# The bank that carries four of the seven products, and one pair more done by seven products

## The chip, the cores and the metric

The kernel runs on one core of one Trainium2 chip. The metric is the device time of one execution in microseconds; before the change three runs gave 1723.54, 1724.14 and 1728.85 us, median 1724.14.

## What is computed

Two layers of an encoder trunk over 512 positions of width 1024. Each layer is a block of four token mixers with a gated sum and an output projection, and then a SwiGLU feed-forward of inner width 2816. Only the feed-forward changes:

```
h2 = rmsnorm(x, ln_ffn[l])
g_part, u_part = jnp.split(h2 @ w_gate_up[l], 2, axis=-1)
x = x + (jax.nn.silu(g_part) * u_part) @ w_down[l]
```

All is float32 in and out. TensorE's operands are float32r, so each matrix is split into a high and a low part (the high part by ScalarE's copy, L121, the low part by VectorE's subtraction, L122), and each product is the sum of three matmuls: high·high, high·low, low·high.

## The kernel before

The activations lie transposed, features on partitions and the 512 positions in the free dimension. The inner width 2816 is 22 tiles of 128. For each tile j the kernel makes a **pair**: the gate tile and the up tile, each 128 x 512, and from them silu(gate)·up, split into ah and al. After pairs 0 to 7, 8 to 15 and 16 to 21 (three groups) the 8 output tiles of the down projection each take their sum over the group's pairs into bank d, and VectorE adds d to x.

The string SEVEN says how pair j is made. An **ordinary** pair (`eight`) is two products of a 128 x 1024 weight tile with all of h: 48 matmuls of 512 columns. A pair **by seven** (`seven`) takes gate and up as two block rows, the contraction's two halves as block columns, and h as 2 x 2 blocks (halves of the contraction by halves of the positions), and forms the result of the eight block products from seven, with sums of weight blocks (s1 to s4) and of blocks of h (T1 to T4): 7 products of 4 x 3 matmuls of 256 columns, 84 in all. In both versions a11·B11 is part of three of the four results. The products go to three PSUM banks, which the traces call fa (r1), fb (r2) and fc (r3).

`sums(j)` loads and prepares the weights of a pair by seven: raw holds a11 and a12 (L1076), s31 is loaded plainly (L1078) and then added to in place by a second DMA, issued by POOL (L1081), and a22 is loaded (L1080). VectorE adds s24 from s31 and raw in two instructions. The splits are called `one` (from raw), v24 (from s24), v1 and v3 (the two halves of s31) and v22 (from a22). s31 and raw have two buffers each, so the load of pair n+2 waits until the last reader of pair n's tile is done; for s31 that is the split v3. In the trace s31, s24 and their splits appear as s_f, the splits of halves as vh_f and vl_f, of whole tiles as wh_f and wl_f.

`seven(j)` doesn't end its own pair: its last two products, a22·T4 and s4·B22, and what follows them are kept as `finish` and run by `rest()` in the middle of the next pair, or at the end of a group. Engines are in order. A scheduler orders the instructions of each engine when the kernel is built, by its own estimates and with `sums` raised in priority by AHEAD instructions, so where an instruction ends up isn't where the code has it.

Of the kernel before, what the change touches and what calls it, by code (L numbers as in the profile page):

```python
# [11 lines left out]
F32 = mybir.dt.float32  # L12
# [3 lines left out]
AF = mybir.ActivationFunctionType  # L16
# [3 lines left out]
P = 128  # L20
S = 512
# [7 lines left out]
LOG_EXP = "natural_log_exp_and_others"  # L29
WL, WR = 3, 2  # L30
LAYERS = range(L)
SEVEN = "8888887777777777777777"
AHEAD = 156
ORDER = "ccbccchhhchhcbchcghcchcchzccczccbccccccchgcgccchbbbcbhcgbzcbbcbccbgghcbgcgcbcccghchghchzhbccccbccccgcccccczhgcgbgchcgcccccccggggggbgcggggbcbbggcbbcbhcccbccbccccccccccccccccccbchccgbgggbchcbbbbbbhbbb"
PE = 8
# [27 lines left out]
def body(tc, io):  # L63
    nc = tc.nc
    V, A, T = nc.vector, nc.scalar, nc.tensor
# [5 lines left out]
    with pool("const") as cl, pool("hp") as hp, pool("wp", WL) as wp, pool("vals", side="right") as cp, \  # L71
# [30 lines left out]
        def tmp(shape, tag="t", dt=F32, bufs=None, name="t"):  # L102
            return tp.tile(shape, dt, tag=tag, name=name, bufs=bufs)

        def acc_psum(name="g"):
            return pm.tile([P, S], F32, tag="mm", name=name)
# [7 lines left out]
        def mul(out, a, b):  # L114
            V.tensor_tensor(out, a, b, op=ALU.mult)

        def add(out, a, b):
            V.tensor_tensor(out, a, b, op=ALU.add)  # L118

        def split(hi, lo, src):  # L120
            A.activation(hi, src, AF.Copy)  # L121
            V.tensor_tensor(lo, src, hi.bitcast(F32), op=ALU.subtract)  # L122
# [78 lines left out]
        def gemm(w, hh, hl, name, ready=None):  # L201
            hi, lo = ready or weight(w, 1024, name)
            ps = acc_psum(name)
            for k in range(KD):
                c = slice(k * P, (k + 1) * P)
                mm3(ps, hi[:, c], lo[:, c], hh[k], hl[k], k == 0, k == KD - 1)
            return ps
# [19 lines left out]
        for l in LAYERS:  # L227
# [14 lines left out]
            with pool(f"mo{l}") as mo, pool(f"mx{l}") as mp:  # L242
# [52 lines left out]
                for nm, c0 in (("m", PK_MR), ("d", PK_DR)):  # L295
                    t = cp.tile([P, 2, NT, 2, 32], F32, tag="rot" + nm, name=f"rot{nm}{l}")
# [715 lines left out]
                for nt in range(KD):  # L1012
                    ps = gemm(io["w_o"][l, nt], mh, ml, f"o{nt}", wo.get(nt))
# [6 lines left out]
            with pool(f"fa{l}") as fa, pool(f"ff{l}") as fp, ps_pool(f"fr{l}", 2) as fr:  # L1020
                tc.keep_in_program_order(nc.scalar.preload_act_table_set(LOG_EXP))
                hh, hl, scale, _ = prenorm(pk[:, PK_FFN:PK_FFN + 8], f"f{l}")
                H, Q = S // 2, KD // 2
# [29 lines left out]
                def moving(b, k):  # L1053
                    if b < 4:
                        return th[k][:, b], tl[k][:, b]
                    k, c = ((k, slice(0, H)), (k + Q, slice(0, H)), (k + Q, slice(H, S)))[b - 4]
                    return hh[k][:, c], hl[k][:, c]

                T1, T2, T3, T4, B11, B21, B22 = range(7)

                def product(ps, w, b, first):
                    for k in range(Q):
                        c = slice(k * P, (k + 1) * P)
                        bh, bl = moving(b, k)
                        for n, (lh, rh) in enumerate(((w[0], bh), (w[0], bl), (w[1], bh))):
                            T.matmul(ps[:, :H], lh[:, c], rh, start=first and k == 0 and n == 0,  # L1066
                                     stop=k == Q - 1 and n == 2, skip_group_check=True)
# [39 lines left out]
                def rest():  # L1107
                    for f in left:
                        f()
                    left.clear()  # L1110

                def hidden(j, g, u, sign=1.0):

                    V.scalar_tensor_tensor(u, u, sign, g, op0=ALU.mult, op1=ALU.mult)
                    ah[j] = fa.tile([P, S], F32R, tag=f"ah{j % 8}", name=f"ah{j}")
                    al[j] = fp.tile([P, S], F32R, tag=f"al{j % 8}", name=f"al{j}")
                    split(ah[j], al[j], u)

                def seven(j):
                    a11, a12, a22, s1, s2, s3, s4 = sums(j)  # L1120
                    gs = fp.tile([P, S], F32, tag="gs", name="gs")
                    us = fp.tile([P, S], F32, tag="us", name="us", bufs=2)
                    r1 = acc_psum(f"fa{j}")
                    product(r1, a11, B11, True)
                    c1 = tmp([P, H], "ps", name="c1")
                    A.activation(c1, r1[:, :H], AF.Copy)
                    rest()
                    r2 = fr.tile([P, S], F32, tag="r2", name=f"fb{j}")
                    r3 = acc_psum(f"fc{j}")
                    uu = tmp([P, 2, H], "n0", name="uu", bufs=1)  # L1130
                    product(r2, s2, T2, True)
                    add(uu[:, 0], c1, r2[:, :H])
                    product(r3, s1, T1, True)
                    product(r1, a12, B21, False)
                    A.activation(gs[:, :H], r1[:, :H], AF.Silu)
                    product(r2, s3, T3, False)
                    add(uu[:, 1], c1, r2[:, :H])
                    add(us[:, H:], uu[:, 1], r3[:, :H])

                    def finish():  # L1140
                        product(r2, a22, T4, False)
                        add(us[:, :H], c1, r2[:, :H])
                        product(r3, s4, B22, False)
                        add(gs[:, H:], uu[:, 0], r3[:, :H])
                        A.activation(gs[:, H:], gs[:, H:], AF.Silu)
                        hidden(j, gs, us, -1.0)

                    left.append(finish)

                def eight(j):  # L1150

                    t = [fp.tile([P, S], F32, tag=n, name=n, bufs=b) for n, b in (("gs", 1), ("us", 2))]
                    pr = []
                    for i in range(2):
                        if 2 * j + i < len(raw):
                            mul(t[i], raw[2 * j + i], r)
                            pr.append(t[i])
                        else:
                            pr.append(gemm(half_gu(2 * j + i), hh, hl, f"f{2 * j + i}"))
                        rest()  # L1160
                    A.activation(t[0], pr[0], AF.Silu)
                    if pr[1] is not t[1]:
                        mul(t[1], pr[1], t[0])
                        ah[j] = fa.tile([P, S], F32R, tag=f"ah{j % 8}", name=f"ah{j}")
                        al[j] = fp.tile([P, S], F32R, tag=f"al{j % 8}", name=f"al{j}")
                        split(ah[j], al[j], t[1])
                    else:
                        hidden(j, t[0], t[1])

                def half_gu(i):  # L1170
                    return io["w_gu"][l, i // 2, :, i % 2 * D:(i % 2 + 1) * D]
# [7 lines left out]
                for k0 in range(0, KF, 8):  # L1179
                    m = min(8, KF - k0)  # L1180
                    for j in range(k0, k0 + m):
                        (seven if SEVEN[j] == "7" else eight)(j)
                        if j < Q:
                            right_sums(j, r)
                    rest()
                    for nt in range(KD):
                        ps = acc_psum(f"d{nt}")
                        hi, lo = weight(io["w_d"][l, nt, :, k0 * P:(k0 + m) * P], m * P, f"d{nt}")
                        for j in range(m):
                            c = slice(j * P, (j + 1) * P)  # L1190
                            mm3(ps, hi[:, c], lo[:, c], ah[k0 + j], al[k0 + j], j == 0, j == m - 1)
                        add(x[nt], x[nt], ps)
                        if k0 + m == KF:
                            nc.sync.dma_start((io["out"] if l == L - 1 else xs)[nt], x[nt])
# [45 lines left out]
def layout(inp):  # L1240
# [9 lines left out]
    def tiles(a, n):  # L1250
# [18 lines left out]
    gu = gu.transpose(0, 2, 3, 1, 4).reshape(L, KF, P, 4, D // 2)  # L1269
    o["w_gu"] = np.stack([gu[:, j][:, :, [1, 0, 2, 3] if SEVEN[j] == "7" else [0, 1, 2, 3]]  # L1270
                          for j in range(KF)], 1).reshape(L, KF, P, 2 * D)
# [41 lines left out]
```

## Time and profile before

| what | value |
|---|---|
| median of three runs | 1724.14 us |
| the profiled execution | 1724.95 us |
| its span, first to last instruction | 1723.2 us |
| instructions | 25722 |
| TensorE's granted clock in the feed-forward stage, 655 to 730 us | 1.00 |
| first matmul of the feed-forward in layer 0 | at 511.87 us |
| pairs by seven | 16 a layer, 32 in all |

The page gives busy time by engine; "idle before" is time in which an engine waited, with what ended most of the wait. A matmul's duration overlaps the next one's, since they are pipelined: how fast TensorE works is read from the distance between starts. In a timeline row the first number is the start in us, the second the duration, and a bracket holds the idle time before it and what released it. SPq and POOLq are the queues that issue DMAs.

### The profile page before, as it was taken

What the parts mean: (1) busy time and instruction counts of PE and PEld (TensorE: products, weight loads), DVE (VectorE), ACT (ScalarE), POOL (GpSimd) and SP (SyncE); (2) the same over time, 40 slices, a digit from 0 to 9 for tenths busy, and PEclk for the clock granted to TensorE, in tenths of its full rate; (3) what the DMA queues carried; (4) which work ended last, traced back from release to release, by engine and by line L of the source; (5) the groups of instructions that cost most, each with busy time, mean ns of one, the idle gap of its engine ahead of it and who ended that gap; (6) DMA issues with size and microseconds to landing.
All of it is one profiled execution on the core that took longest, in us unless ns stands there. A gap on an engine that the chain in (4) does not pass through costs nothing.

```text
span 1723.2 us, 25722 instructions
## 1 busy us (share of the span) xinstructions
PE 1697.8 (99%) x10220; PEld 1422.5 (83%) x10220; DVE 1179.0 (68%) x1979; ACT 808.8 (47%) x1352; POOL 43.0 (2%) x68
## 2 busy tenths in 40 slices
PE   8999999999999999999999999999999999999999
PEld 6787778877787989989887777788777788899897
DVE  8858775457769647748677687754667695487473
ACT  7374353456555424525453743534564453254251
POOL 1000000000000000000000000000000000000000
PEclk9999999999999999999999999999999999999999
DMA  5222203332262435644442221142323624365443
GB/s 193 64 80 86 74 26 115 105 99 86 87 201 100 138 110 161 170 122 126 133 136 58 87 74 62 43 119 97 110 75 111 189 87 140 118 177 145 127 115 104
DMA packets 62473, 191.58 MB, mean 111 GB/s; under 512 B 7953, under 2 KB 9361, under 8 KB 62353
## 3 DMA queue, kind: packets, MB, share of 16 engines
q1 hardware_dynamic: 56304, 170.10, 30.4%
q0 software_dynamic: 5760, 19.42, 6.2%
q8 instruction: 80, 1.31, 0.3%
q10 hardware_dynamic: 288, 0.43, 0.1%
q14 instruction: 41, 0.33, 0.1%
HBM read 179.42 MB, written 4.19 MB: 107 GB/s over the span
## 4 chain that ended last, share of the span: by engine, by line
PE 87%; DVE 7%; ACT 3%; DMA 2%; issue 1%; SPq 0%; POOLq 0%; ACTq 0%; DVEq 0%
PE fb L1066 8%; PE g L142 6%; PE g L141 6%; PE g L143 6%; PE fc L1066 5%; PE fa L1066 5%; PE d L141 5%; PE d L143 5%; PE d L142 5%; PE f L142 3%; PE f L141 3%; PE f L143 3%; DMA s_f<-in_w_gu 2%; PE av L942 1%; PE sm L909 1%; PE hf L142 1%
## 5 line engine op out<-in xcount | busy, mean ns | idle before, releaser
L141 PE MATMUL g<-hhm,wh_g 128*128 128x512 f32 x512 | 202.0, 394 | 0.0
L143 PE MATMUL g<-hhm,wl_g 128*128 128x512 f32 x512 | 201.5, 394 | 0.0
L142 PE MATMUL g<-hlm,wh_g 128*128 128x512 f32 x512 | 201.5, 394 | 0.0
L143 PE MATMUL d<-ah,wl_d 128*128 128x512 f32 x352 | 136.9, 390 | 0.5 <-DVE wl_d L122 0.5
L141 PE MATMUL d<-ah,wh_d 128*128 128x512 f32 x352 | 137.2, 392 | 0.0
L142 PE MATMUL d<-al,wh_d 128*128 128x512 f32 x352 | 137.1, 390 | 0.0
L122 DVE TENSOR_TENSOR wl_g<-wr_g,wh_g 128x1024 fp32r<-128x1024 f32 x64 | 78.3, 1223 | 73.8 <-ACT wh_g L121 73.8
L121 ACT ACTIVATE wh_g<-wr_g 128x1024 fp32r<-128x1024 f32 x64 | 67.7, 1058 | 115.4 <-PE g L142 80.1
L142 PEld LDWEIGHTS g<-hlm,wh_g 128*128 128x128 f32 x512 | 96.3, 188 | 20.4 <-issue 1.5
L141 PEld LDWEIGHTS g<-hhm,wh_g 128*128 128x128 f32 x512 | 96.3, 188 | 20.2 <-issue 0.8
L143 PEld LDWEIGHTS g<-hhm,wl_g 128*128 128x128 f32 x512 | 96.3, 188 | 20.0 <-issue 0.8
L121 ACT ACTIVATE wh_d<-wr_d 128x1024 fp32r<-128x1024 f32 (+1 forms) x48 | 47.5, 989 | 111.7 <-PE d L142 85.5
L118 DVE TENSOR_TENSOR xm<-xm,d 128x512 f32<-128x512 f32 x48 | 33.0, 688 | 88.9 <-PE d L143 88.8
L121 ACT ACTIVATE wh_f<-wr_f 128x1024 fp32r<-128x1024 f32 x50 | 53.0, 1059 | 79.1 <-PE d L142 35.0
L121 ACT ACTIVATE vh_f<-s_f 128x512 fp32r<-128x512 f32 x64 | 40.1, 630 | 103.4 <-PE fb L1066 63.8
L910 DVE TENSOR_REDUCE nm<-sm 128x1 f32<-128x512 f32 x64 | 43.8, 689 | 51.3 <-PE sm L909 50.9
L143 PEld LDWEIGHTS d<-ah,wl_d 128*128 128x128 f32 x352 | 66.1, 188 | 14.9 <-DVE wl_d L122 1.4
L141 PEld LDWEIGHTS d<-ah,wh_d 128*128 128x128 f32 x352 | 66.0, 188 | 14.9 <-ACT ah L121 1.9
L142 PEld LDWEIGHTS d<-al,wh_d 128*128 128x128 f32 x352 | 66.1, 188 | 14.0 <-DVE al L122 1.2
L1066 PE MATMUL fb<-th,vh_f 128*128 128x256 f32 x256 | 75.7, 296 | 0.4 <-DVE uu L118 0.3
L1066 PE MATMUL fa<-hhf,wl_f 128*128 128x256 f32 x256 | 72.7, 284 | 0.0
L1066 PE MATMUL fa<-hlf,wh_f 128*128 128x256 f32 x256 | 72.5, 283 | 0.0
(444 smaller groups left out, 4845.6 us busy)
## 6 DMA issues: line engine op xcount, KB each, us to landing
wr_g<-in_w_g SPq DMA_DIRECT2D x64, 512.0 KB, 3.6
wr_f<-in_w_gu SPq DMA_DIRECT2D x50, 512.0 KB, 3.5
s_f<-in_w_gu SPq DMA_DIRECT2D x32, 512.0 KB, 4.5
s_f<-in_w_gu POOLq DMA_DIRECT2D x32, 512.0 KB, 5.4
wr_d<-in_w_d SPq DMA_DIRECT2D x32, 512.0 KB, 3.5
wr_b<-in_w_b SPq DMA_DIRECT2D x16, 512.0 KB, 3.4
wr_o<-in_w_o SPq DMA_DIRECT2D x16, 512.0 KB, 3.5
a_f<-in_w_gu SPq DMA_DIRECT2D x32, 256.0 KB, 3.0
```

The costliest lines, as they stand in the source:

```text
L118: V.tensor_tensor(out, a, b, op=ALU.add)
L121: A.activation(hi, src, AF.Copy)
L122: V.tensor_tensor(lo, src, hi.bitcast(F32), op=ALU.subtract)
L141: T.matmul(ps, lh, rh, start=first, stop=False)
L142: T.matmul(ps, lh, rl, start=False, stop=False)
L143: T.matmul(ps, ll, rh, start=False, stop=last)
L909: T.matmul(ps, qs[0:96, t * P:(t + 1) * P], ks[0:96], start=True, stop=True)
L910: V.tensor_reduce(nm[:, j:j + 1], ps, axis=AX.X, op=ALU.max, negate=True)
L942: T.matmul(av[e * 64:e * 64 + 64], vv[:, b, 2 * i + e], pts[i][e][:, b].rearrange("p t q -> p (t q)"), start=t == 1 and b == 0, stop=b == ...
L1066: T.matmul(ps[:, :H], lh[:, c], rh, start=first and k == 0 and n == 0, stop=k == Q - 1 and n == 2, skip_group_check=True)
```

## The change

One more pair by seven: pair 5 of each layer. In `seven`, bank r2 now starts with a11·B11 and then gathers s2·T2, s3·T3 and a22·T4 without being started anew; ScalarE copies it out after each step (c1, cc[:, 0], cc[:, 1], and us[:, :H] at the end), where VectorE added c1 to it three times. a12·B21 goes alone to r1, and VectorE adds c1 to it before Silu. r2 is now taken before `rest()`, and s2·T2 comes after it. The tile gs has two buffers instead of one, us one instead of two.

```diff
--- before.py
+++ after.py
@@ -29,7 +29,7 @@
 LOG_EXP = "natural_log_exp_and_others"
 WL, WR = 3, 2
 LAYERS = range(L)
-SEVEN = "8888887777777777777777"
+SEVEN = "8888877777777777777777"
 AHEAD = 156
 ORDER = "ccbccchhhchhcbchcghcchcchzccczccbccccccchgcgccchbbbcbhcgbzcbbcbccbgghcbgcgcbcccghchghchzhbccccbccccgcccccczhgcgbgchcgcccccccggggggbgcggggbcbbggcbbcbhcccbccbccccccccccccccccccbchccgbgggbchcbbbbbbhbbb"
 PE = 8
@@ -1118,30 +1118,31 @@
 
                 def seven(j):
                     a11, a12, a22, s1, s2, s3, s4 = sums(j)
-                    gs = fp.tile([P, S], F32, tag="gs", name="gs")
-                    us = fp.tile([P, S], F32, tag="us", name="us", bufs=2)
+                    gs = fp.tile([P, S], F32, tag="gs", name="gs", bufs=2)
+                    c1 = tmp([P, H], "ps", name="c1")
                     r1 = acc_psum(f"fa{j}")
-                    product(r1, a11, B11, True)
-                    c1 = tmp([P, H], "ps", name="c1")
-                    A.activation(c1, r1[:, :H], AF.Copy)
+                    r2 = fr.tile([P, S], F32, tag="r2", name=f"fb{j}")
+                    product(r2, a11, B11, True)
+                    A.activation(c1, r2[:, :H], AF.Copy)
+                    product(r1, a12, B21, True)
+                    add(gs[:, :H], c1, r1[:, :H])
+                    A.activation(gs[:, :H], gs[:, :H], AF.Silu)
                     rest()
-                    r2 = fr.tile([P, S], F32, tag="r2", name=f"fb{j}")
+                    cc = tmp([P, 2, H], "n0", name="cc", bufs=1)
                     r3 = acc_psum(f"fc{j}")
-                    uu = tmp([P, 2, H], "n0", name="uu", bufs=1)
-                    product(r2, s2, T2, True)
-                    add(uu[:, 0], c1, r2[:, :H])
+                    product(r2, s2, T2, False)
+                    A.activation(cc[:, 0], r2[:, :H], AF.Copy)
                     product(r3, s1, T1, True)
-                    product(r1, a12, B21, False)
-                    A.activation(gs[:, :H], r1[:, :H], AF.Silu)
                     product(r2, s3, T3, False)
-                    add(uu[:, 1], c1, r2[:, :H])
-                    add(us[:, H:], uu[:, 1], r3[:, :H])
+                    A.activation(cc[:, 1], r2[:, :H], AF.Copy)
+                    us = fp.tile([P, S], F32, tag="us", name="us")
+                    add(us[:, H:], cc[:, 1], r3[:, :H])
 
                     def finish():
                         product(r2, a22, T4, False)
-                        add(us[:, :H], c1, r2[:, :H])
+                        A.activation(us[:, :H], r2[:, :H], AF.Copy)
                         product(r3, s4, B22, False)
-                        add(gs[:, H:], uu[:, 0], r3[:, :H])
+                        add(gs[:, H:], cc[:, 0], r3[:, :H])
                         A.activation(gs[:, H:], gs[:, H:], AF.Silu)
                         hidden(j, gs, us, -1.0)
 
@@ -1149,7 +1150,7 @@
 
                 def eight(j):
 
-                    t = [fp.tile([P, S], F32, tag=n, name=n, bufs=b) for n, b in (("gs", 1), ("us", 2))]
+                    t = [fp.tile([P, S], F32, tag=n, name=n, bufs=b) for n, b in (("gs", 2), ("us", 1))]
                     pr = []
                     for i in range(2):
                         if 2 * j + i < len(raw):
```

Outside the feed-forward, and up to pair 5 in it, every engine has the same order as before. Two places show what moved inside.

The first is VectorE in the middle of pairs 8 to 15 of layer 0. vl_f11, vl_f12 on s31 are the low parts of the splits v1 and v3 of pairs 11 and 12 (the second of a pair is v3), s24_f13 are the two adds of pair 13. Before (the split v3 of pair 11 stands six rows above the first row shown):

```order
L118 TENSOR_TENSOR s24_f12_6399<-s24_f12_6399,wr_f12_6388 128x512
L118 TENSOR_TENSOR us_6151<-uu_6201,fc10_6200 128x256
L118 TENSOR_TENSOR us_6151<-c1_6165,fb10_6199 128x256
L122 TENSOR_TENSOR vl_f12_6407<-s31_f12_6390,vh_f12_6406 128x512
L118 TENSOR_TENSOR gs_6150<-uu_6201,fc10_6200 128x256
L118 TENSOR_TENSOR uu_6335<-c1_6299,fb11_6333 128x256
L122 TENSOR_TENSOR wl_f12_6396<-wr_f12_6388,wh_f12_6395 128x1024
L122 TENSOR_TENSOR vl_f12_6411<-s31_f12_6390,vh_f12_6410 128x512
L1114 SCALAR_TENSOR_TENSOR us_6151<-us_6151,gs_6150 128x512
L122 TENSOR_TENSOR wl_f12_6403<-s24_f12_6399,wh_f12_6402 128x1024
L122 TENSOR_TENSOR vl_f12_6415<-a22_f12_6392,vh_f12_6414 128x512
L118 TENSOR_TENSOR s24_f13_6533<-s31_f13_6524,wr_f13_6522 128x512
```

Now (the first row is the split v3 of pair 11, and right behind the last row comes vl_f12_6482, the split v3 of pair 12):

```order
L122 TENSOR_TENSOR vl_f11_6347<-s31_f11_6326,vh_f11_6346 128x512
L122 TENSOR_TENSOR al9_6279<-us_6187,ah9_6278 128x512
L122 TENSOR_TENSOR vl_f11_6351<-a22_f11_6328,vh_f11_6350 128x512
L118 TENSOR_TENSOR us_6322<-cc_6282,fc10_6283 128x256
L118 TENSOR_TENSOR gs_6354<-c1_6355,fa11_6356 128x256
L122 TENSOR_TENSOR wl_f12_6467<-wr_f12_6459,wh_f12_6466 128x1024
L122 TENSOR_TENSOR vl_f12_6478<-s31_f12_6461,vh_f12_6477 128x512
L118 TENSOR_TENSOR gs_6219<-cc_6282,fc10_6283 128x256
L122 TENSOR_TENSOR wl_f12_6474<-s24_f12_6470,wh_f12_6473 128x1024
L1114 SCALAR_TENSOR_TENSOR us_6322<-us_6322,gs_6219 128x512
L118 TENSOR_TENSOR s24_f13_6605<-s31_f13_6596,wr_f13_6594 128x512
L118 TENSOR_TENSOR s24_f13_6605<-s24_f13_6605,wr_f13_6594 128x512
```

Before, v3 of pair 12 (vl_f12_6411) stood ahead of the first s24 add of pair 13; now both adds stand ahead of it. The three rows that follow v3 (al, the split of a22, and the add into us[:, H:]) follow it again after pair 12. The adds of uu are gone, and gs has taken an add of c1 and bank fa.

The second is ScalarE at the same place. vh and wh are the high parts of the splits, c1 and cc the copies of the bank. Before:

```order
L121 ACTIVATE vh_f11_6280<-a22_f11_6258 128x512
L1126 ACTIVATE c1_6299<-fa11_6286 128x256
L121 ACTIVATE vh_f12_6406<-s31_f12_6390 128x512
L121 ACTIVATE wh_f12_6395<-wr_f12_6388 128x1024
L1145 ACTIVATE gs_6150<-gs_6150 128x256
L121 ACTIVATE vh_f12_6410<-s31_f12_6390 128x512
L121 ACTIVATE wh_f12_6402<-s24_f12_6399 128x1024
L121 ACTIVATE ah10_6329<-us_6151 128x512
L121 ACTIVATE vh_f12_6414<-a22_f12_6392 128x512
L1135 ACTIVATE gs_6284<-fa11_6286 128x256
L1126 ACTIVATE c1_6433<-fa12_6420 128x256
```

Now:

```order
L1126 ACTIVATE c1_6355<-fb11_6357 128x256
L121 ACTIVATE wh_f12_6466<-wr_f12_6459 128x1024
L1129 ACTIVATE gs_6354<-gs_6354 128x256
L121 ACTIVATE vh_f12_6477<-s31_f12_6461 128x512
L1143 ACTIVATE us_6322<-fb10_6222 128x256
L121 ACTIVATE wh_f12_6473<-s24_f12_6470 128x1024
L1146 ACTIVATE gs_6219<-gs_6219 128x256
L1134 ACTIVATE cc_6417<-fb11_6357 128x256
L121 ACTIVATE vh_f12_6481<-s31_f12_6461 128x512
L121 ACTIVATE ah10_6413<-us_6322 128x512
L121 ACTIVATE vh_f12_6485<-a22_f12_6463 128x512
L1137 ACTIVATE cc_6417<-fb11_6357 128x256
```

Per pair there was one copy (c1); now there are four (c1, us, and cc twice). The copy to cc[:, 0] stands behind the split of s24 and the second Silu, the copy to cc[:, 1] behind the split of a22.

On TensorE the products of a pair now stand whole behind each other, 12 matmuls each: a11·B11, a12·B21, then a22·T4 and s4·B22 of the pair before, then s2·T2, s1·T1, s3·T3. Before they were a11·B11, s2·T2 (in part, or with a part of s1·T1), a22·T4 and s4·B22 of the pair before, the rest of s2·T2 and s1·T1, a12·B21, s3·T3. At the end of a group 4 matmuls of the down projection stand between s3·T3 and a22·T4, and 6 did before. SP issues the loads of a pair in the same order as before: raw, s31, a22.

## Prediction

> **What bounds the kernel now.** I read the page first, for the engine that is never idle, then the chain that ended last, then the timelines of the feed-forward stage, the only stage whose order changes.
>
> ```profile
> PE 1697.8 (99%) x10220; PEld 1422.5 (83%) x10220; DVE 1179.0 (68%) x1979; ACT 808.8 (47%) x1352; POOL 43.0 (2%) x68
> PE 87%; DVE 7%; ACT 3%; DMA 2%; issue 1%; SPq 0%; POOLq 0%; ACTq 0%; DVEq 0%
> 655.00:730.00 75.00, 74.42 (x591) 72.19 (x591) 58.76 (x95) 38.20 (x63) 5.23 (x6) 1.00 0.64 170
> ```
>
> TensorE is busy for 99% of the span and owns 87% of the chain. In 75 us of seven-product pairs (third row: PE, PEld, DVE, ACT, POOL busy, clock, DMA share, GB/s) it is busy for 74.4; VectorE has 58.8 (78%), ScalarE 38.2 (51%), at a granted clock of 1.00. So time is won only by fewer or denser matmuls, and lost wherever something makes PE wait.
>
> Two rates follow. In an ordinary pair, from the start of the first row below to that of the second, 27 matmuls of 512 columns are issued in 6.12 us, 0.227 us each. In a seven, the chain shows 12 matmuls of 256 columns, one product, in 1.44 us, 0.120 each.
>
> ```profile
> 540.63 0.39 PE L141 MATMUL f<-hhf,wh_f 128*128 128x512 f32 x1
> 546.75 0.39 PE L141 MATMUL f<-hhf,wh_f 128*128 128x512 f32 x1
> ...
> 671.88 1.44 PE fa L1066 x12
> 682.20 1.44 PE fa L1066 x12
> 692.40 1.44 PE fa L1066 x12
> 702.67 1.44 PE fa L1066 x12
> ```
>
> The fa rows are a11·B11 of four pairs in turn: (702.67 - 671.88) / 3 = 10.26 us a pair, while 7 products of 1.44 us are 10.08. The 0.18 us left over is a wait in each pair:
>
> ```profile
> 685.31 0.42 DVE L118 TENSOR_TENSOR uu<-c,fb 128x256 f32<-128x256 f32 x1
> 685.63 0.28 PE L1066 MATMUL fc<-th,vh_f 128*128 128x256 f32 x1
> 685.78 0.39 PE L1066 MATMUL fb<-th,vh_f 128*128 128x256 f32 x1
> 686.01 0.28 PE L1066 MATMUL fb<-tl,vh_f 128*128 128x256 f32 x1
> ```
>
> a22·T4 may not add to bank fb before VectorE has read uu from it (ended 685.73); PE starts at 685.78, and the next matmul comes 0.23 later instead of 0.12, a restart of about 0.1.
>
> **The change part by part.** *One pair more by seven products.* 48 x 0.227 = 10.90 us become 84 x 0.120 = 10.08: -0.82 a layer, -1.6 in all.
>
> *Copies on ScalarE for adds on VectorE.* Per pair VectorE loses two adds of 0.42, and ScalarE gains three copies. The copy of today:
>
> ```profile
> 683.67 0.38 ACT L1126 ACTIVATE c<-fa 128x256 f32<-128x256 f32 x1 [0.61 <-PE fa L1066]
> 687.40 0.63 ACT L121 ACTIVATE vh_f<-s_f 128x512 fp32r<-128x512 f32 x1 [3.34 <-PE fb L1066]
> 688.84 1.06 ACT L121 ACTIVATE wh_f<-wr_f 128x1024 fp32r<-128x1024 f32 x1 [0.81 <-PE fc L1066]
> 690.32 0.40 ACT L1145 ACTIVATE gs<-gs 128x256 f32<-128x256 f32 x1
> ```
>
> With 3 x 0.38 more per 10.08, ScalarE goes from 51% to some 62%: room enough. The tightest copy is cc[:,0]: only s1·T1, 1.44 us, stands between the end of s2·T2 and s3·T3 on the same bank. Count from the end of a pair's s3·T3 (block ends at 1.44, 2.88 ...). By the new order ScalarE does the split of s24 after s4·B22 (5.76): 5.84 to 6.90, Silu to 7.30, and the copy 0.2 after s2·T2 ends at 7.20: 7.40 to 7.78. PE wants it at 8.64. So the per-pair wait should go: 32 x 0.19 = -6.1 us. What is late next decides the case.
>
> *The order on VectorE, which the scheduler drew anew.* Before, the split v3 of pair n+1 stands ahead of the s24 adds of pair n+2; now it stands right behind them (order rows above). These adds need s31 of pair n+2, which is loaded and then added to in place by POOL's DMA, into the buffer of pair n (two buffers), so not before v3 of pair n is done. What was a loop over two pairs is now one over a single pair: v3 of n, load, adding load, two s24 adds, v3 of n+1. Its terms:
>
> ```profile
> 670.07 0.69 DVE L122 TENSOR_TENSOR vl_f<-s_f,vh_f 128x512 fp32r<-128x512 f32 x1
> 683.51 0.69 DVE L118 TENSOR_TENSOR s_f<-s_f,wr_f 128x512 f32<-128x512 f32 x1
> 684.11 0.69 DVE L122 TENSOR_TENSOR al<-us,ah 128x512 fp32r<-128x512 f32 x1
> 640.55 1.42 DVE L118 TENSOR_TENSOR s_f<-s_f,wr_f 128x512 f32<-128x512 f32 x2
> ...
> 649.39 0.33 SPq L1078 DMA_DIRECT2D s_f<-in_w_gu  x1
> 670.78 0.33 SPq L1078 DMA_DIRECT2D s_f<-in_w_gu  x1
> 680.62 1.15 SPq L1078 DMA_DIRECT2D s_f<-in_w_gu  x1
> 711.03 0.33 SPq L1078 DMA_DIRECT2D s_f<-in_w_gu  x1
> 776.32 0.33 SPq L1078 DMA_DIRECT2D s_f<-in_w_gu  x1
> ...
> 653.92 0.86 POOL L1081 DMA_DIRECT2D s_f<-in_w_gu  x1 [20.99 <-DMA s_f<-in_w_gu]
> 675.91 0.88 POOL L1081 DMA_DIRECT2D s_f<-in_w_gu  x1 [9.89 <-DVE us L118]
> 686.91 0.87 POOL L1081 DMA_DIRECT2D s_f<-in_w_gu  x1 [10.13 <-DMA s_f<-in_w_gu]
> 715.81 0.87 POOL L1081 DMA_DIRECT2D s_f<-in_w_gu  x1 [7.58 <-DMA s_f<-in_w_gu]
> 780.30 0.87 POOL L1081 DMA_DIRECT2D s_f<-in_w_gu  x1 [19.07 <-DVE uu L118]
> ...
> s_f<-in_w_gu POOLq DMA_DIRECT2D x7, 512.0 KB, 5.2
> ```
>
> v3 of pair 11 ends at 670.76 and SP issues at 670.78, so the trigger is direct; today its data is used 12.8 us after v3, at 683.51, and nobody waits. From SP's issue to POOL's the five rows give 4.53, 5.13, 6.29, 4.78 and 3.98 us; the slow ones have a weight load issued just ahead of them, which the new order doesn't have there, so I take 4.7. POOL's DMA lands 5.2 us after its start. The pair of adds and v3 are 1.42 + 0.69 less the 0.09 by which neighbours on VectorE overlap (683.51 to 684.11 is 0.60, for 0.69 each): 2.02. With 0.09 for the two hand-overs, **the loop is 12.0 us, while PE needs a pair every 10.08**: VectorE, in order, falls behind by 1.9 us a pair.
>
> Who feels it? Behind v3 of n+1 stand two splits and us[:, H:] of pair n, which must leave bank fc before s4·B22 of pair n overwrites it: -0.09 + 0.60 + 0.60 + 0.42 + 0.05 = 1.58 us after v3's end. Count a group from its first a11·B11. Its first pair has five products (7.2 us), and s4·B22 of its k-th pair (k = 0 first) wants to start at 7.20 + 10.08 k + 4.32. The first link, v3 of the second pair, waits for s1·T1 of the first (5.76); today that split ends 1.28 after it:
>
> ```profile
> 646.65 1.44 PE fc L1066 x12
> 648.68 0.69 DVE L122 TENSOR_TENSOR vl_f<-s_f,vh_f 128x512 fp32r<-128x512 f32 x1 [1.49 <-ACT vh_f L121]
> ```
>
> (fc ends at 648.09, the split at 649.37.) With the s24 adds now ahead of it I take 7.3. Pairs 8 to 15: us of pair 13 hangs on five links, 7.3 + 60 + 1.58 = 68.9, against 7.20 + 50.4 + 4.32 = 61.9 for its s4·B22: **7.0 us late**. Later pairs of the group have no adds ahead of their v3 and lose no more. Pairs 16 to 21: three links, 44.9 against 41.8: **3.1 late**. Pairs 5 to 7: their only such load is set off before the first seven, so nothing. Both layers: 2 x 10.1 = +20.2 us; in general 16 x loop - 171.8.
>
> *Small costs.* In the first pair of each layer cc[:,0] stands behind a split that waits for s1·T1 and, in layer 0, behind a table load:
>
> ```profile
> 575.06 1.28 ACT L1161 ACT_TABLE_LOAD   x1
> ```
>
> I take 1.3 + 0.7 = 2.0, between nothing and 4. At the end of a group 4 ordinary matmuls, not 6, part s3·T3 from a22·T4: 0.9 us, where split and copy on ScalarE need 1.1: 0.2 x 6 = 1.2. Twelve waits with a restart of 0.1: 1.2. The second us buffer becomes a second gs buffer: no wait in the rows hangs on it, so nothing.
>
> Sum: -1.6 - 6.1 + 20.2 + 2.0 + 1.2 + 1.2 = +16.9 on the profiled execution's 1724.95, that is 1741.9. The median of the three runs is 0.8 lower, so I say **1741 us**.
>
> The Trainium skill, page "DMA: Bandwidth & Descriptors", section on the anatomy of one DMA on the gpsimd path, fits a DMA as 2.0 us plus its bytes over 436 GB/s; by it POOL's 512 KB would take an estimated 3.2 us, the loop would be 10.0, and there would be no lag at all (the first rival's time). The trace disagrees: 5.2 us. The row decides.
>
> **Rivals.** *The load loop hides in slack.* If the two transfers came in 8.0 us or less instead of 9.9, the loop would fit into 10.08 and the 20.2 and the restarts would go: -1.6 - 6.1 + 2.0 + 1.2 = -4.5, so 1720; without the small costs 1717. For it: fewer loads overlap at that place. Against: the quickest chain above is 3.98 + 5.2 = 9.2. *The chain at its quickest.* 9.2 makes the loop 11.3, and the lag 9.0: 1730, at the edge of what can be told. *ScalarE is the bound.* cc[:,0] has 0.86 us to spare; it stands behind Silu, which waits for VectorE's gs add. Were that add 1.4 us late in all 34 pairs, s3·T3 would wait 0.5 each: +17 in place of the 20.2, 1737. Against it: by the new order the add's forerunner, the split v1, ends at about 5.97, when s4·B22 (5.76 + 0.2) has just come out, so the add is prompt. *The copies don't free PE*: with the wait of 0.18 kept, 6 more than the forecast, 1747; against it stand the 0.86 and the 1.8 us to spare of the other copies.
>
> **How the numbers follow.** Forecast, loop binding at 11.5 to 13: 0.72. Hidden: 0.10. Quickest chain: 0.10. ScalarE or kept waits: 0.08. The range: a chain of 9.2 to 11 (the third pair above, 6.29 + 5.2, is over that, but has SP issuing late) gives loops of 11.3 to 13.1, lags of 9.0 to 37.8, times of 1730 to 1759; I reach down to 1728 to cover part of the hidden case and cut at 1754. Within 0.3% is about what a measurement can tell from no change: 1719 to 1729. The hidden case gives half of its chance to faster and half to same, the quickest chain half to same and half to slower, the others all to slower: faster 0.05, same 0.10, slower 0.85.
>
> **What would show it.** Right: VectorE idle for 2 to 3 us before s_f<-s_f,wr_f, released by DMA, and PE idle before fc, released by VectorE's us, from about the third pair of pairs 8 to 15 and of 16 to 21, with the pairs 12 us apart; no waits before fb in between; pairs 14 and 15 back at 10.08. Wrong: adds with no idle time, pairs at 10.1 to 10.3 throughout, or PE waiting before fb for ScalarE's cc.

## The result

| what | before | after |
|---|---|---|
| median, run side by side | 1724.35 us | 1753.19 us |
| ratio, 95% interval | | 1.016, 1.0146 to 1.0174 |
| span of the profiled execution | 1723.2 us | 1754.2 us |
| pairs by seven in a layer | 16 | 17 |

The changed kernel is 1.6% slower: 28.8 us, where the forecast said 17 and its range ended at 30. One of the six runs of the changed kernel took 2767.26 us at a granted clock of 0.557; it counts in the median and not in the ratio, and without it the median is 1752.61. First the page of the profile of after: busy time by engine, the chain that ended last, the group of the s24 adds (the right column is the idle time of VectorE ahead of them), and the two loads of s31.

```profile
PE 1704.4 (97%) x10292; PEld 1434.1 (82%) x10292; DVE 1162.2 (66%) x1931; ACT 848.8 (48%) x1464; POOL 44.4 (3%) x70
...
PE 82%; DVE 8%; issue 3%; ACT 3%; DMA 2%; SPq 0%; DVEq 0%; ACTq 0%; POOLq 0%
...
L118 DVE TENSOR_TENSOR s_f<-s_f,wr_f 128x512 f32<-128x512 f32 x68 | 47.0, 691 | 77.5 <-issue 60.1
...
s_f<-in_w_gu SPq DMA_DIRECT2D x34, 512.0 KB, 3.6
s_f<-in_w_gu POOLq DMA_DIRECT2D x34, 512.0 KB, 6.9
```

TensorE's share falls from 99% to 97% of a longer span, and of the chain from 87% to 82%. VectorE stands idle for 77.5 us ahead of the s24 adds; in the kernel before it was 15.6:

```profile
L118 DVE TENSOR_TENSOR s_f<-s_f,wr_f 128x512 f32<-128x512 f32 x64 | 44.0, 688 | 15.6 <-DMA wr_f<-in_w_gu 15.2
```

Where TensorE waits, the view of waits shows, for the stages from 500 us on (total, number of waits, the longest):

```profile
PE fc L1066 <- DVE us L118: 26.3, 13, 3.8
```

That is the wait the prediction named: s4·B22 wants bank fc, and VectorE's add into us has not read it yet. The view has one wait before fb, of 0.2 us. In the kernel before it has one too, of 0.3, so it doesn't show the 0.18 us in each pair that the prediction counted; the distance of the pairs does. In the first two pairs of pairs 8 to 15, s3·T3 and, right behind it and also into fb, a11·B11 of the next pair start at:

```profile
651.07 2.88 PE fb L1066 x24
...
661.15 2.88 PE fb L1066 x24
```

That is 10.08 us apart, the seven products and nothing more; the waits before fb are gone there. The 75 us that the prediction read for before read now (PE, PEld, DVE, ACT, POOL busy, clock, DMA share, GB/s):

```profile
655.00:730.00 75.00, 66.75 (x525) 65.94 (x524) 47.16 (x72) 40.63 (x75) 5.16 (x6) 0.95 0.58 152
```

TensorE is busy for 66.8 us instead of 74.4; ScalarE, which took over the copies, is at 54%, far from a bound. VectorE's timeline in pairs 8 to 15 of layer 0 has the loop itself: v3 (the split whose end frees the buffer), the idle time ahead of the adds of the pair after next, the adds, and the next v3.

```profile
651.84 0.68 DVE L122 TENSOR_TENSOR vl_f<-s_f,vh_f 128x512 fp32r<-128x512 f32 x1
...
663.46 0.68 DVE L122 TENSOR_TENSOR vl_f<-s_f,vh_f 128x512 fp32r<-128x512 f32 x1
...
675.62 1.42 DVE L118 TENSOR_TENSOR s_f<-s_f,wr_f 128x512 f32<-128x512 f32 x2 [4.44 <-issue]
676.96 0.68 DVE L122 TENSOR_TENSOR vl_f<-s_f,vh_f 128x512 fp32r<-128x512 f32 x1
...
678.77 0.41 DVE L118 TENSOR_TENSOR us<-cc,fc 128x256 f32<-128x256 f32 x1
...
716.96 0.68 DVE L122 TENSOR_TENSOR vl_f<-s_f,vh_f 128x512 fp32r<-128x512 f32 x1
```

From the first v3 to the last are five links: (716.96 - 651.84) / 5 = **13.0 us a link**, where 12.0 was forecast and TensorE needs 10.08. The 4.44 us before the adds carry the word "issue" and not DMA, but the next two views give the reason. First the timeline of SP and POOL in the same link, then the DMA view of the moment in which POOL issues (KB, and us from issue to landing):

```profile
664.17 0.33 SPq L1078 DMA_DIRECT2D s_f<-in_w_gu  x1
...
667.73 0.33 SPq L1076 DMA_DIRECT2D wr_f<-in_w_gu  x1
...
667.78 0.86 POOL L1081 DMA_DIRECT2D s_f<-in_w_gu  x1 [10.22 <-DVE wl_f L122]
```

```profile
s_f<-in_w_gu POOLq DMA_DIRECT2D x1, 512.0 KB, 7.8
```

v3 ends at 664.14, SP issues at 664.17, POOL 3.61 later, its adding load lands 7.8 us after that, at about 675.6, and the adds start at 675.62. The row of POOL names VectorE's wl_f as what released it. But SP's load lands 3.1 us after its issue, at 667.27, and POOL starts 0.5 us behind that, as in the next two links (0.5 and 0.6), so the landing is the likelier cause. The link is closed as forecast, but with 7.8 us for the adding load, not 5.2: the load of the next pair's first weight tile (wr_f) is issued right beside it, at 667.73. On TensorE's side the chain of waits shows s4·B22 of pair 10 and of pair 13:

```profile
679.23 2.45 PE fc L1066 x12
...
719.24 1.70 PE fc L1066 x12
```

(719.24 - 679.23) / 3 = 13.3 us a pair.

### The profile page after: what moved, and what is told of

Same layout as the page of the kernel before. It is cut to its first block, busy times and chain, and to the rows that moved or that the text cites. A ratio compares the mean times of both kernels' runs of the same rounds, so it can differ in the third digit from the quotient of the medians.

```text
span 1754.2 us, 26009 instructions
## 1 busy us (share of the span) xinstructions
PE 1704.4 (97%) x10292; PEld 1434.1 (82%) x10292; DVE 1162.2 (66%) x1931; ACT 848.8 (48%) x1464; POOL 44.4 (3%) x70
## 4 chain that ended last, share of the span: by engine, by line
PE 82%; DVE 8%; issue 3%; ACT 3%; DMA 2%; SPq 0%; DVEq 0%; ACTq 0%; POOLq 0%
PE fb L1066 9%; PE g L142 6%; PE g L141 6%; PE g L143 6%; PE fc L1066 5%; PE d L142 5%; PE d L141 5%; PE d L143 5%; PE f L142 3%; PE f L141 3%; PE f L143 3%; PE fa L1066 2%; DMA s_f<-in_w_gu 2%; PE o L142 1%; PE av L942 1%
## 5 line engine op out<-in xcount | busy, mean ns | idle before, releaser
L141 PEld LDWEIGHTS g<-hhm,wh_g 128*128 128x128 f32 x512 | 96.3, 188 | 20.2 <-issue 0.8
L118 DVE TENSOR_TENSOR s_f<-s_f,wr_f 128x512 f32<-128x512 f32 x68 | 47.0, 691 | 77.5 <-issue 60.1
L1066 PE MATMUL fb<-tl,vh_f 128*128 128x256 f32 x272 | 76.9, 283 | 0.0
L1066 PE MATMUL fb<-th,vl_f 128*128 128x256 f32 x272 | 76.9, 283 | 0.0
```

The source lines that it names most:

```text
L141: T.matmul(ps, lh, rh, start=first, stop=False)
```

## The experiments

Two theories stood from the start. *The load loop*: the order in which VectorE now does the s24 adds and v3 turns loading into a loop over one pair. *The new scheme itself*: the copies on ScalarE, the bank held through four products, or the pair more. The edits below are against the changed kernel.

**One pair more, done the old way (e2).** This edit alone is against the kernel before:

```diff
-SEVEN = "8888887777777777777777"
+SEVEN = "8888877777777777777777"
```

> The old way of doing a pair by seven (one copy c1, added three times on VectorE), with pair 5 done by seven too: only the string SEVEN is that of the change. VectorE's order keeps the split v3 of a pair ahead of the s24 adds of the next. Theory (the load loop costs the time, the extra pair gains 0.8 us a layer): 1724.35 - 1.6 + 2 x 0.19 for the wait kept in two pairs more = about 1723, between 1721 and 1727, with no idle VectorE before the s24 adds. Rival (a pair more by seven is what costs, since its loads and splits come on top): 1735 or more.

Measured: 1724.03 us, ratio to the kernel before 0.9998 (0.9989 to 1.0007). A pair more by seven does not cost; that it gains 1.6 us is within the interval, and the times say no more. One profile of each says a little more: from the first matmul of the feed-forward's first gate product (tile fr) to the first of pair 8, the kernel before takes 125.01 us in layer 0 and 125.05 in layer 1, this one 124.23 and 124.44. That is 0.8 and 0.6 us less, where 0.82 a layer was forecast. Ahead of the s24 adds VectorE stands idle for 14.4 us in all, nearly as before (15.6).

**The new way, with the old count (e3).**

```diff
-SEVEN = "8888877777777777777777"
+SEVEN = "8888887777777777777777"
```

> The new way of doing a pair by seven (one bank through four products, copied by ScalarE), with the old string SEVEN, so pair 5 is ordinary. In VectorE's order the s24 adds of pair n+2 stand ahead of the split v3 of pair n+1, as in the changed kernel. Theory (the load loop): about 1.6 slower than the changed kernel or equal to it within 4 us, so 1750 to 1757, with the links about 13 us apart and PE waiting before fc for VectorE's us. Rival (the pair more costs): about 1724.

Measured: 1754.92 us, ratio 1.0186 (1.0168 to 1.0204). The whole loss is there without the pair more: it comes with the new scheme. TensorE's wait for VectorE's us is there too, in its view of waits:

```profile
PE fc L1066 <- DVE us L118: 23.2, 12, 3.5
```

**Only the order of the adds put back (e4, and e10 once more).** A constraint keeps the two s24 adds behind the split v3 of the pair before; nothing else is touched. The edit in part (the lines that keep hold of v3's split are not shown):

```diff
+                        with tc.issue_after(v3_low[-1].ins) if v3_low else nullcontext():
-                        add(s24[:, :512], s31[:, 512:], raw[:, 512:])
-                        add(s24[:, 512:], s24[:, :512], raw[:, :512])
+                            add(s24[:, :512], s31[:, 512:], raw[:, 512:])
+                            add(s24[:, 512:], s24[:, :512], raw[:, :512])
```

> The changed kernel with one constraint on the order of VectorE: the two s24 adds of a pair stand behind the split v3 of the pair before, as they did before the change. All else (copies on ScalarE, the one bank, 17 pairs a layer) stays. Theory (only the order of these adds costs the time): the loop runs over two pairs again and goes, and what is left is -1.6 - 6.1 and small costs of up to 4.4: 1717 to 1722, faster than both kernels, with PE waiting neither before fc nor before fb, and a clock of 1.00 in the seven-product stage. Rival A (the copies on ScalarE or the bank held through four products cost the time): stays at 1745 or more. Rival B (the waits before fb were hidden cost only and come back elsewhere): 1724 to 1728.

Measured: 1719.73 us, ratio 0.9976 (0.9963 to 0.9988), and in a second measurement of five rounds:

> The kernel e4 once more, in more rounds, on the same chip as e9 and the kernel before: 1717 to 1722, faster than the kernel before by 0.2 to 0.4%.

1719.85 us, ratio 0.9966 (0.9954 to 0.9979). Here the place of these adds in VectorE's order is the one thing that differs from the changed kernel (in the traces every other engine has the same order in both), and the 33 us go with it. This version is faster than both kernels, by 0.2 to 0.3% in the case of the one before. Its window of the same stage, and, in the view by lines, what is left of the idle time ahead of the s24 adds:

```profile
655.00:730.00 75.00, 75.00 (x606) 73.73 (x604) 56.26 (x84) 47.02 (x88) 6.03 (x7) 1.00 0.65 176
```

```profile
L119 DVE TENSOR_TENSOR s_f<-s_f,wr_f 128x512 f32<-128x512 f32 x68 | 46.8, 688 | 21.7 <-DMA wr_f<-in_w_gu 14.4 <-DMA s_f<-in_w_gu 6.8
```

TensorE is busy without a gap, 75.00 of 75, at a clock of 1.00. The chain has a12·B21 of pair 9 and of pair 15 at:

```profile
652.87 1.44 PE fa L1067 x12
...
713.35 1.44 PE fa L1067 x12
```

(713.35 - 652.87) / 6 = 10.08 us a pair, where the kernel before has 10.26: the wait in each pair is gone.

**No weight load beside POOL's (e5).** Pairs 10 to 15 and 18 to 21 take the raw tile of the pair two before, so that 20 loads of 512 KB are left out; the order of the adds stays as in the changed kernel. The edit in part:

```diff
+                        if j in (10, 11, 12, 13, 14, 15, 18, 19, 20, 21):
+                            raw = raws[j % 2]
+                        else:
+                            raw = raws[j % 2] = rp.tile([P, 1024], F32, tag="wr", name=f"wr_f{j}")
+                            nc.sync.dma_start(raw, src[:, :1024])
```

> The changed kernel, but pairs 10 to 15 and 18 to 21 load no first weight tile (wr_f) of their own; they use that of the pair two before, so part of the weights is wrong and 20 loads of 512 KB are left out. VectorE's order, with the s24 adds ahead of v3, stays. In the changed kernel POOL's adding load takes 6.2 to 8.4 us where wr_f is issued up to 1.4 us ahead of it or with it, 5.3 where it comes 1.0 later. Theory (the loop binds, and its adding load is slow because the weight load is issued beside it): POOL's load lands after 5.0 to 5.5 us, links of 3.6 + 5.2 + 2.1 = 10.9 us (10.7 to 11.4) in place of 13.0; by 16 x loop - 171.8 that is 0 to 11 us late in both layers, so 1720 to 1732. Rival A (the adding load is slow for another reason, as that it follows the plain load of the same tile more closely): 6.5 to 7.5 us, links of 12.5 or more, 1745 to 1753. Rival B (the loop isn't what sets the time): no change, 1753, whatever the load takes.

Measured: 1743.15 us, ratio 1.0091 (1.0068 to 1.0113). The adding load did what was expected; below are the medians from 640 to 700 us, first of the changed kernel, then of this one:

```profile
s_f<-in_w_gu POOLq DMA_DIRECT2D x4, 512.0 KB, 7.0
```

```profile
s_f<-in_w_gu POOLq DMA_DIRECT2D x4, 512.0 KB, 5.3
```

but the time fell by 10 us, not by 20 to 33. The link was reckoned too short: v3 of the first and of the last link,

```profile
650.09 0.68 DVE L122 TENSOR_TENSOR vl_f<-s_f,vh_f 128x512 fp32r<-128x512 f32 x1
...
709.39 0.68 DVE L122 TENSOR_TENSOR vl_f<-s_f,vh_f 128x512 fp32r<-128x512 f32 x1
```

are 59.3 us apart, 11.9 a link. The expectation had taken the quickest 3.6 us from SP to POOL for all links, where these have 3.7 to 4.4, and had forgotten that the last link of a group has a load of the down projection's weights beside it: POOL's load takes 7.1 us in that of this group.

All 16 links of both layers make 193.05 us here, 12.1 each. By the prediction's formula that is 193.05 - 171.8 = 21.3 us late, and with its 1.2 for the restarts 22.5; against e4 the cost is 1743.15 - 1719.73 = 23.4. That 12.1 is nearly the 12.0 of the prediction is luck: in the mean it is 4.1 us from SP to POOL and 5.8 for the adding load, where the prediction had 4.7 and 5.2. So the loop costs over 1% even without loads of wr_f beside POOL's, and these loads make the rest: 1753.19 - 1743.15 = 10 us.

**The idle time of TensorE filled with work (e6).**

```diff
+                        if j in (10, 11, 12, 13, 18, 19):
+                            idle = sc_psum("idle")
+                            for n in range(12):
+                                T.matmul(idle, s4[0][:, :P], hh[n % KD], start=n == 0, stop=n == 11,
+                                         skip_group_check=True)
                         product(r3, s4, B22, False)
```

> The changed kernel with 12 matmuls of 512 columns, whose result nobody reads, ahead of s4.B22 of pairs 10 to 13, 18 and 19, where TensorE waits 2.0 to 3.8 us for VectorE's us: 12 x 0.227 = 2.7 us of work in place of idle time, 32.6 us of added matmuls in all. Theory (the load loop is the clock of these pairs and TensorE only waits there): the matmuls cost nearly nothing, 1750 to 1757, with the links at 13 us as before. Rival (TensorE's own work sets the distance of the pairs): 1753 + 33 = 1785. On the granted clock, which fell to 0.5 for 3.4 us five times in the seven-product stages of the changed kernel and never in those of the kernel before: if idle TensorE brings the falls, there are none or one here; if they come by chance or with the new order of products, four to six.

Measured: 1753.03 us, ratio 1.0163 (1.0147 to 1.0179). 144 matmuls more cost nothing, so TensorE does not set the distance of the pairs in these groups. And the clock stays at full speed. The windows of the changed kernel first, then of this one:

```profile
680.00:690.00 10.00, 10.00 (x73) 10.00 (x73) 5.26 (x8) 5.39 (x11) 0.87 (x1) 0.84 0.60 146
...
700.00:710.00 10.00, 6.23 (x41) 6.03 (x41) 7.20 (x12) 3.63 (x6) 0.86 (x1) 0.86 0.41 127
```

```profile
680.00:690.00 10.00, 10.00 (x83) 9.91 (x83) 5.48 (x9) 5.82 (x11) 0.86 (x1) 1.00 0.58 143
...
700.00:710.00 10.00, 10.00 (x75) 9.51 (x74) 7.84 (x12) 4.64 (x9) 0.87 (x1) 1.00 0.50 143
```

**Four ordinary pairs, with the adds put back (e7).** Beside the edit of e4:

```diff
-SEVEN = "8888877777777777777777"
+SEVEN = "8888777777777777777777"
```

> The kernel with the s24 adds put behind v3 of the pair before (e4), and with pair 4 done by seven as well: four ordinary pairs first. By the rate of the matmuls 0.82 us a layer less: 1719.7 - 1.6 = 1718, between 1715 and 1721, and then faster than the kernel before by 0.3 to 0.4%. Rival (the first pairs by seven lack something, as their T blocks or the first loads, since they come 10 us sooner): 1721 to 1728, with waits of TensorE in pairs 4 and 5.

Measured: 1730.70 us, ratio 1.003 (1.0019 to 1.0042): the rival, and beyond it. The view of waits of TensorE from 500 us on, and the window in which the first pair by seven of layer 0 is under way:

```profile
PE fb L1067 <- ACT wh_f L122: 4.5, 3, 2.3
PE fc L1067 <- DVE us L119: 2.6, 3, 1.3
PE fc L1067 <- DVE tl L123: 1.7, 2, 0.9
```

```profile
565.70:572.30 6.60, 5.95 (x26) 5.66 (x27) 5.22 (x17) 2.72 (x4) 0.86 (x1) 0.50 0.79 199
```

The T blocks (tl) and the splits of pair 4 come too late, TensorE stands still, and its clock is then at half speed for a while, in both layers. For this order four ordinary pairs are too few.

**The adds put back, with the old count (e9).** Beside the edit of e4:

```diff
-SEVEN = "8888877777777777777777"
+SEVEN = "8888887777777777777777"
```

> The changed kernel with the s24 adds put behind v3 of the pair before, and with the old string SEVEN: pair 5 is ordinary. The new bank alone, without the loop. Theory: what e4 gains against the kernel before (5.0 us) comes from the waits before fb, 32 x 0.19 = 6.1, less small costs; the pair more adds its 0.8 a layer, so here 1719.7 + 1.6 = 1721.3, between 1719 and 1724. Rival (the gain of e4 hangs on the pair more): 1724 to 1727.

Measured: 1724.62 us, ratio 0.9994 (0.9985 to 1.0003), a miss: it is the time of the rival, by which the gain of e4 hangs on the pair more. Its eleven runs lie between 1720.74 and 1726.24, and the profiled one has 7.9 us of a wait that is 0.5 us in e4's second profile; then VectorE's timeline, where the first of these waits comes from:

```profile
PE fc L1067 <- DVE us L119: 7.9, 5, 2.5
```

```profile
670.51 0.69 DVE L119 TENSOR_TENSOR s_f<-s_f,wr_f 128x512 f32<-128x512 f32 x1 [0.30 <-DMA s_f<-in_w_gu]
...
684.40 0.69 DVE L119 TENSOR_TENSOR s_f<-s_f,wr_f 128x512 f32<-128x512 f32 x1 [4.11 <-DMA s_f<-in_w_gu]
```

So with the adds behind v3 the loads still have less than a microsecond to spare in a pair (in e4 the load that POOL issues at 685.17 lands 5.4 us later, 0.9 ahead of the add at 691.50), and one late load makes VectorE wait in the next. Pairs 8 to 15 with their down projection take 127.45 and 128.67 us in the two layers of this profile, 124.64 and 124.67 in e4's first one; these 6.8 us are more than the 6.1 by which the two profiled executions differ. That the late loads are the whole cause is argued from one profile. Why they are late here and not in e4 was not found, so the rival is not excluded.

## Why the prediction was right, and where it was short

*What bounds, and what the new order does*: shown. The idle VectorE, TensorE's wait at bank fc from the third pair of pairs 8 to 15 on, the first link (v3 of pair 9 was forecast 7.3 us into the group, which begins at 645.15, and ends at 652.52) and the pairs 10.08 us apart ahead of these waits and behind them (s3·T3 of pairs 14 and 15 at 723.81 and 733.89) are as written, and putting back the one order of e4 removes the loss. The signs were larger than written: VectorE idle for 0.7 to 6.0 us a link, not 2 to 3, and the pairs 13.3 apart, not 12.

*The load loop, +20.2 us*: the mechanism holds, the size was too small. The term that was too small is "POOL's DMA lands 5.2 us after its start". It was read where the next weight load came some 4 us later; I had even taken from the order that no weight load is issued *ahead of s31's plain load* any more, and had lowered SP to POOL to 4.7 for it, but had not asked where that load goes instead. It goes beside POOL's. Measured over the 16 links: 3.6 to 4.6 us from SP to POOL, 4.0 in the mean, and 5.1 to 8.4 for the adding load, 6.65 in the mean; 12.8 together with the rest, in place of 12.0. So the 4.7 was too large by 0.7 and the 5.2 too small by 1.45. The first and the last v3 of the other three groups of links (three, five and three):

```profile
788.77 0.68 DVE L122 TENSOR_TENSOR vl_f<-s_f,vh_f 128x512 fp32r<-128x512 f32 x1
...
826.27 0.69 DVE L122 TENSOR_TENSOR vl_f<-s_f,vh_f 128x512 fp32r<-128x512 f32 x1
...
1519.18 0.68 DVE L122 TENSOR_TENSOR vl_f<-s_f,vh_f 128x512 fp32r<-128x512 f32 x1
...
1583.21 0.68 DVE L122 TENSOR_TENSOR vl_f<-s_f,vh_f 128x512 fp32r<-128x512 f32 x1
...
1657.52 0.68 DVE L122 TENSOR_TENSOR vl_f<-s_f,vh_f 128x512 fp32r<-128x512 f32 x1
...
1696.00 0.69 DVE L122 TENSOR_TENSOR vl_f<-s_f,vh_f 128x512 fp32r<-128x512 f32 x1
```

With the first group the 16 links make 65.1 + 37.5 + 64.0 + 38.5 = 205.1 us; less 171.8 that is 33.3 us late, in the prediction's own formula, and with its 1.2 for the restarts 34.5. The changed kernel and e4, which differ in nothing but this loop, lie 1753.19 - 1719.73 = 33.5 apart. The formula was right to 1 us, and two durations in it were wrong, by 0.8 a link together. The measured time is 0.8 us inside the range, which the prediction had cut at 1754 though its own slowest chain led to 1759; that it came out inside is luck.

*The rest of the sum*, -1.6 - 6.1 + 2.0 + 1.2 = -4.5: e4 is the kernel in which only these terms act, and it lies 5.0 under the kernel before in both measurements (1724.72 and 1724.85 beside it). Together they hold, singly not all of them. The wait in each pair is gone (10.08 for 10.26), and the pair more shows in e2's profile, if not in its time; but e9, without the pair more, didn't come out faster. The 2.0 us of the first pairs did not come. TensorE's waits before fb and fc from 500 us on are, in e4's first profile and then in its second:

```profile
PE fc L1067 <- DVE us L119: 2.3, 2, 1.4
...
PE fb L1067 <- ACT cc L1140: 0.2, 1, 0.2
...
PE fc L1067 <- DVE us L119: 0.5, 1, 0.5
...
PE fb L1067 <- ACT cc L1140: 0.2, 1, 0.2
```

The 0.2 is the first pair by seven of layer 0; that of layer 1 has no such wait. The waits before fc stand in pairs 16 to 21, where in the first profile a load of s31 is late, and the sum had nothing for them.

*The rivals.* "Hides in slack" is what e4 shows (1720 forecast, 1719.73 measured), for another order. "The chain at its quickest", 9.2 us, came in two of the 16 links only (9.1 and 9.5). "ScalarE is the bound" and "the copies don't free PE" fall with the pairs at 10.08 and the one wait of 0.2 us before fb; ScalarE is busy for 47.0 of the 75 us of e4's window, 63%, where some 62% was forecast. The Trainium skill's page "DMA: Bandwidth & Descriptors", section on the anatomy of one DMA on the gpsimd path, whose fit gave an estimated 3.2 us for POOL's load and with it no lag, is not borne out here either: 6.9 us is the median of the changed kernel.

## What to carry to other kernels

When a scheduler draws an order anew, look for the instruction that frees a buffer and for the one that waits for the next load into it, and count over how many iterations the loop through the buffer now runs; one swap of two neighbours can halve that number. A duration from the old trace holds only in the old company: for each load in such a loop ask what will be issued beside it in the new order, since a load that leaves one place turns up at another. And measure the change with the old order forced back before judging its idea: here the bank and the pair more gain 0.2 to 0.3% together (the bank without the pair more, in e9, nothing that could be told from none), and the order lost 1.9%.

## What the runs showed of the hardware

*Of two loads side by side, mostly the one that comes second pays.* Before the change, POOL's adding load of 512 KB takes 5.2 us in the median between 655 and 700 us, where weight loads come some 4 us behind it. In the changed kernel, at 667.78 and 0.05 us behind a load of wr_f, it takes 7.8 and that load 3.6. In e4, where wr_f comes 1.2 to 1.7 us behind POOL, the adding load keeps its time and wr_f pays; medians of e4 between 660 and 700 us:

```profile
s_f<-in_w_gu POOLq DMA_DIRECT2D x4, 512.0 KB, 5.3
wr_f<-in_w_gu SPq DMA_DIRECT2D x3, 512.0 KB, 5.1
```

The Trainium skill, page "DMA: Bandwidth & Descriptors", section "Queues, rings and completion order", says that each DMA engine takes turns between the queues, packet by packet. By even turns both loads would be stretched alike. Here the larger part mostly falls on the later one: in the other links of the changed kernel in which SP's load is 0.6 to 1.4 us ahead, it takes 3.2 to 5.0 us and POOL's 6.1 to 8.4. There are exceptions. In e4 a load of wr_d of 384 KB comes 0.40 us behind POOL's of 800.98 and takes 4.2 us, and POOL's takes 8.1. In e5 two adding loads of layer 1 took 6.6 and 6.9 us with no weight load beside them, so the company is not the only cause.

*A wait of about 2 us can bring half the clock for 3.4 us.* After the wait at 679.23 the windows of the changed kernel read (clock is the third number from the right):

```profile
679.23 0.39 PE L1066 MATMUL fc<-hhf,wh_f 128*128 128x256 f32 x1 [2.25 <-DVE us L118]
```

```profile
676.40:679.80 3.40, 1.15 (x9) 0.95 (x9) 3.40 (x7) 0.38 (x2) 0.00 (x0) 1.00 0.29 99
679.90:683.20 3.30, 3.30 (x18) 3.30 (x17) 2.37 (x4) 2.21 (x5) 0.87 (x1) 0.50 0.78 245
683.40:686.80 3.40, 3.40 (x30) 3.40 (x30) 1.03 (x2) 1.67 (x4) 0.00 (x0) 1.00 0.94 175
```

Not every such wait does it: ahead of the matmul at 1572.10 TensorE stands still for 2.22 us, and from 1573.0 to 1580.0 the clock is 1.00. In e6, with the waits filled, no window of this stage is under 1.00. The Trainium skill, page "TensorE: Matmul & The Clock Gate", Part 1, tells of a free-running window of 3.4 us after which an idle array is throttled. The length agrees; but here 2.25 us without a matmul, not a whole window, was enough. In the changed kernel these falls cost little, as e6 shows, since TensorE was waiting for VectorE anyway.
